# Expert retrieval in a hybrid diffusion layer: index masks from one VectorE comparison, in place of a GpSimd subtraction and two ScalarE steps

## The chip, the cores and the metric

The kernel runs on one core of a Trainium2 chip. The metric is the device time of one execution, in microseconds (us). Three runs of the kernel before took 3352.09, 3352.52 and 3352.99 us; the median is 3352.52 us.

The engines are named as the profile names them: PE is TensorE (matmuls), DVE is VectorE, ACT is ScalarE, POOL is GpSimd, SP is SyncE.

## The reference

The program computes one layer over 512 latent tokens of width 2048 with 256 context tokens: modulated RMS norm, a combined projection into attention heads and gated short convolutions, an output projection with a gated residual, and then a product-key retrieval of experts. The change lies in the retrieval, which the reference computes like this, for blocks of 128 tokens:

```python
def block(hb):                                           # PEER_HEADS = 8, PEER_TOPK = 16, N_KEYS = 128
    q = (hb @ w_pq).reshape(nb, PEER_HEADS, 2, PEER_QDIM // 2)
    s = jnp.einsum('nhpd,hpkd->nhpk', q, sub_keys).astype(jnp.float32)
    s_top, i_top = lax.top_k(s, PEER_TOPK)
    cand = s_top[:, :, 0, :, None] + s_top[:, :, 1, None, :]
    cand_idx = i_top[:, :, 0, :, None] * N_KEYS + i_top[:, :, 1, None, :]
    best_s, best_pos = lax.top_k(cand.reshape(nb, PEER_HEADS, PEER_TOPK * PEER_TOPK), PEER_TOPK)
    expert = jnp.take_along_axis(cand_idx.reshape(nb, PEER_HEADS, PEER_TOPK * PEER_TOPK), best_pos, axis=-1)
    gate = jax.nn.softmax(best_s, axis=-1).astype(hb.dtype).reshape(nb, PEER_HEADS * PEER_TOPK)
    expert = expert.reshape(nb, PEER_HEADS * PEER_TOPK)
    act = jax.nn.gelu(jnp.einsum('nd,ned->ne', hb, u_tab[expert]), approximate=False) * gate
    return jnp.einsum('ne,ned->nd', act, v_tab[expert])
```

The step that changes is `take_along_axis`: for each of the 16 best candidates of a head it picks the expert's index.

## The kernel before

Each fp32 product is made of three matmuls (`mm3`, L106 to L109): weights come as tiles of 128 x 1024 fp32, ACT rounds them to a high part `whi` (L102), DVE subtracts to get the low part `wlo` (L103), and PE needs both. There are four buffers each for `raw`, `whi` and `wlo`. The `wlo` of one half tile of every second query is made on POOL in place of DVE (the argument `eng` in `query`).

The retrieval begins about 1063 us into the span. There are 16 queries, two for each of 8 heads. `query(c)` makes 128 features of one half of a head for all 512 tokens (PE, 48 matmuls of 512 columns into `qps`), `half_top` multiplies them with the 128 sub-keys (`scp`, L556), copies the scores to SBUF on ACT (`sc`, L558), and finds the 16 best of each token with the DVE's max, index and replace instructions (L563 to L567). `head_top` adds the two halves' values and indices for the 50 pairs that can be among the 16 best (L582; NP = 50), finds the 16 best pairs (L590 to L594), and has their positions as floats in `posf` (L595). All this is done for four groups of 128 tokens (t = 0 to 3), tokens on partitions.

To turn a position into an expert's index the kernel makes, for each head and each t, a tile `hit` of 128 x (16 x 50): POOL subtracts the position from an iota 0 to 49 (L599); ACT squares it (L607) and takes max(0, 1 - x) (L608), which is 1 where the position matches and 0 elsewhere; POOL multiplies with the candidates' indices `cidx`, the second half of `both` (L609); DVE sums over the 50 (L613). In the loop at the end of the section, the subtraction of a head is issued with its `head_top`, `hit_masks` two queries later, and `hit_sums` a query after that. The order of instructions on each engine is set by the framework's scheduler, under the marks `issue_after`; each engine then runs its list in that order. There are eight `hit` buffers, two heads' worth.

After the queries PE goes on to 128 blocks of dense scores against the table u (`u_block`, 48 matmuls of 352 columns into `sps`, two tiles of `wlo` each), the first few of them still in the same loop, while DVE finishes the last heads and the softmax of the gates (`gates`, L616 to L625). Expert indices of the last 160 tokens go to POOL, which gathers rows by indirect DMA (L728). The rest of the program, some 2000 us, goes over the tables u and v at the pace of PE.

Of the kernel before, what the change touches and what calls it, by code (L numbers as in the profile page):

```python
# [10 lines left out]
F32 = mybir.dt.float32  # L11
# [3 lines left out]
AF = mybir.ActivationFunctionType  # L15
ALU = mybir.AluOpType
# [4 lines left out]
P = 128  # L21
# [18 lines left out]
NP = len(PAIRS)  # L40


def build(nc, tc, ap, es):
# [269 lines left out]
    with pool("att", side="right", **reuse) as att:  # L313
        bias = [att.tile([P, 512], F32, name=f"bias{i}") for i in range(2)]
# [194 lines left out]
    iota = pq.tile([P, P], F32, name="iota")  # L509
# [4 lines left out]
    tk = tks.enter_context(pool("tk", side="right", **reuse))  # L514

    gate = {}
    mark = {}

    def u_block():
        i = u_block.n  # L520
        u_block.n += 1
        ps = psum("u", "sps", P, ND)
        for hf in range(2):
            w = weights(ap["uT"][i, hf])
            for k in range(8):
                kk = 8 * hf + k
                mm = mm3(ps, (w[0][:, k, :], w[1][:, k, :]), (HH[:, kk, 0:ND], HL[:, kk, 0:ND]), kk == 0, kk == KD - 1)
        mark["pe"], mark["dve"], mark["act"] = mm, weights.lo, weights.hi
        if i % 2 == 0:
            u_block.out = uo.tile([P, 2, ND], F32, tag="ug", bufs=2, name="ug")  # L530
        nc.scalar.activation(u_block.out[:, i % 2, :], ps, AF.Gelu)
        if i % 2 == 1:
            nc.scalar.dma_start(gu[i // 2], u_block.out)
# [3 lines left out]
    def query(c):  # L537
        ps = psum("query", "qps", P, T)
        for hf in range(2):
            w = weights(ap["wpq"][c, hf], nc.gpsimd if c % 2 == 1 and hf == 0 else None)  # L540
            for k in range(8):
                kk = 8 * hf + k
                mm = mm3(ps, (w[0][:, k, :], w[1][:, k, :]), h2[kk], kk == 0, kk == KD - 1)
            if hf == 0:
                gate["pe"] = mm
        qt = tk.tile([P, T], F32, tag="qt", bufs=3, name="qt")
        gate["act"] = nc.scalar.activation(qt, ps, AF.Copy)
        sk = tk.tile([P, P], F32, tag="sk", bufs=3, name="sk")
        nc.sync.dma_start(sk, ap["skT"][:, c, :])
        return qt, sk  # L550

    def half_top(p, qt, sk):
        sp = psum("scores", "scp", P, 4, P)
        with tc.issue_after(gate["pe"].ins):
            for t in range(4):
                nc.tensor.matmul(sp[:, t, :], qt[:, P * t:P * t + P], sk, start=True, stop=True)  # L556
        sc = tk.tile([P, 4, P], F32, tag="sc", bufs=2, name="sc")
        nc.scalar.activation(sc, sp, AF.Copy)  # L558
        tops = tk.tile([P, 2, 4, 16], F32, tag=f"top{p}", bufs=2, name="tops")
        top = tops[:, 0]  # L560
        idx = tk.tile([P, 4, 16], U32, tag=f"idx{p}", bufs=2, name="idx")
        for t in range(4):
            nc.vector.max(top[:, t, 0:8], sc[:, t, :])  # L563
            nc.vector.max_index(idx[:, t, 0:8], top[:, t, 0:8], sc[:, t, :])
            nc.vector.match_replace(sc[:, t, :], top[:, t, 0:8], sc[:, t, :], NEG)
            nc.vector.max(top[:, t, 8:16], sc[:, t, :])
            nc.vector.max_index(idx[:, t, 8:16], top[:, t, 8:16], sc[:, t, :])  # L567
        if p == 0:
            nc.vector.tensor_scalar(tops[:, 1], idx, P, None, op0=ALU.mult)
        else:  # L570
            nc.vector.tensor_copy(tops[:, 1], idx)
        return tops

    def head_top(hd, first, second):
        both = tk.tile([P, 2, 4, NP], F32, tag="cand", bufs=2, name="both")
        o = 0
        for a in range(9):
            n, na = (16 // (a + 1), 1) if a < 8 else (1, 8)
            dst = both[:, :, :, o:o + n * na]
            x = second[:, :, :, 0:n].to_broadcast([P, 2, 4, n * na]) if na > 1 else second[:, :, :, 0:n]  # L580
            y = first[:, :, :, a:a + na].to_broadcast([P, 2, 4, n * na]) if n > 1 else first[:, :, :, a:a + na]
            nc.vector.tensor_tensor(dst, x, y, op=ALU.add)  # L582
            o += n * na
        cand, cidx = both[:, 0], both[:, 1]
        assert o == NP
        pos = tk.tile([P, 4, 16], U32, tag="pos", bufs=2, name="pos")
        posf = tk.tile([P, 4, 16], F32, tag="posf", bufs=2, name="posf")
        for t in range(4):
            bt = best[:, t, hd, :]
            nc.vector.max(bt[:, 0:8], cand[:, t, :])  # L590
            nc.vector.max_index(pos[:, t, 0:8], bt[:, 0:8], cand[:, t, :])
            nc.vector.match_replace(cand[:, t, :], bt[:, 0:8], cand[:, t, :], NEG)
            nc.vector.max(bt[:, 8:16], cand[:, t, :])
            nc.vector.max_index(pos[:, t, 8:16], bt[:, 8:16], cand[:, t, :])  # L594
        nc.vector.tensor_copy(posf, pos)  # L595
        hits = [None] * 4
        for t in (3, 2, 1, 0):
            hit = tk.tile([P, 16, NP], F32, tag="hit", bufs=8, name="hit")
            nc.gpsimd.tensor_tensor(hit, iota[:, 0:NP].unsqueeze(1).to_broadcast([P, 16, NP]),  # L599
                                    posf[:, t, :].unsqueeze(2).to_broadcast([P, 16, NP]), op=ALU.subtract)  # L600
            hits[t] = hit
        return hd, hits, cidx

    def hit_masks(hd, hits, cidx):
        for t in (3, 2, 1, 0):
            with tc.issue_after(gate["act"].ins):
                nc.scalar.activation(hits[t], hits[t], AF.Square)  # L607
            nc.scalar.activation(hits[t], hits[t], AF.Relu, bias=1.0, scale=-1.0)  # L608
            nc.gpsimd.tensor_tensor(hits[t], hits[t], cidx[:, t, :].unsqueeze(1).to_broadcast([P, 16, NP]), op=ALU.mult)  # L609

    def hit_sums(hd, hits, cidx):
        for t in (3, 2, 1, 0):
            nc.vector.tensor_reduce(expt[:, t, hd, :], hits[t], axis=AX.X, op=ALU.add)  # L613

    def gates():
        for t in range(4):  # L616
            bt = best[:, t]
            mx = pq.tile([P, NH], F32, tag="mx", bufs=2, name="mx")
            nc.vector.tensor_copy(mx, bt[:, :, 0])
            nc.vector.tensor_tensor(bt, bt, mx.unsqueeze(2).to_broadcast([P, NH, 16]), op=ALU.subtract)  # L620
            nc.scalar.activation(bt, bt, AF.Exp)
            sm = pq.tile([P, NH], F32, tag="sm", bufs=2, name="sm")
            nc.vector.tensor_reduce(sm, bt, axis=AX.X, op=ALU.add)
            nc.vector.reciprocal(sm, sm)
            nc.vector.tensor_tensor(bt, bt, sm.unsqueeze(2).to_broadcast([P, NH, 16]), op=ALU.mult)  # L625
# [3 lines left out]
    found = summed = None  # L629
    for c in range(1, 2 * NH + 4):  # L630
        nxt = None
        if c < 2 * NH:
            nxt = query(c)
        else:
            for _ in range(2):
                u_block()
            gate["act"], gate["pe"] = mark["act"], mark["pe"]
        if c == 2 * NH + 1:
            gates()
            u_block()  # L640
        if c % 2 == 1:
            if summed:
                hit_sums(*summed)
            summed = None
        elif found:
            hit_masks(*found)
            summed, found = found, None
        if c <= 2 * NH:
            halves.append(half_top((c - 1) % 2, *qs))
            qs = nxt  # L650
            if c % 2 == 0:
                if c == 2 * NH:
                    u_block()
                found = head_top(c // 2 - 1, *halves)
                halves = []
# [303 lines left out]
```

## Time and profile before

| what | value |
|---|---|
| median of the three runs | 3352.52 us |
| the profiled execution's own time | 3354.18 us |
| its span (first to last instruction) | 3352.3 us |
| PE busy | 3251.0 us, 97% of the span |
| DVE busy | 2494.3 us, 74% |
| ACT busy | 1180.7 us, 35% |
| POOL busy | 674.7 us, 20% |

PE is busy in nearly all of the span, so a stretch is of interest where it is not. A row of the timeline gives start (us from the span's start), duration, engine, line, operation, output and inputs, shapes and count; in square brackets stands how long the engine sat idle before it, and what ended that. An instruction that has started but can't get at its operands shows as a longer duration, not as idle time.

### The profile page before, as it was taken

The page shows a single profiled execution, that of the slowest core. Times are in us where ns is not written, and L with a number is a line of the kernel's source. Part 1 is how long each engine was busy: PE and PEld are TensorE (multiplying, and loading weights), DVE is VectorE, ACT ScalarE, POOL GpSimd, SP SyncE. Part 2 cuts the span into 40 slices and gives each one's busy share as a digit, 9 for nine tenths or more (in the row PEclk, how much of TensorE's full clock was granted, in tenths as well). Part 3 has the DMA queues.
Part 4 walks back from the last instruction along what each step waited for, and adds up shares of the span by engine and source line. Part 5 has one row for each costly group of instructions (what it writes and reads, how often), then busy time and mean ns, then how long its engine had stood idle before and what let it go on. Part 6 is the DMA issues. An engine that isn't in the chain of part 4 may idle for free.

```text
span 3352.3 us, 48155 instructions
## 1 busy us (share of the span) xinstructions
PE 3251.0 (97%) x18951; PEld 2994.3 (89%) x18951; DVE 2494.3 (74%) x3648; ACT 1180.7 (35%) x1584; POOL 674.7 (20%) x400
## 2 busy tenths in 40 slices
PE   4899999999999998999999999999999999999999
PEld 1488888878887888999999999999999999999999
DVE  4444444888756798888788788667688899889885
ACT  3344444322323445333333333323333333333332
POOL 0000000000000465121122221222233333333330
PEclk9999999999999999999999999999999999999999
DMA  8722221788773323889999999998999999999994
GB/s 301 250 68 65 65 62 57 253 276 281 243 251 117 105 86 127 318 330 353 341 346 344 339 336 347 350 351 337 361 357 363 381 369 364 372 377 364 366 346 169
DMA packets 265315, 912.52 MB, mean 272 GB/s; under 512 B 23808, under 2 KB 77312, under 8 KB 222720
## 3 DMA queue, kind: packets, MB, share of 16 engines
q1 hardware_dynamic: 208208, 527.74, 45.1%
q0 software_dynamic: 46080, 335.56, 25.9%
q10 hardware_dynamic: 10800, 46.14, 3.4%
q8 instruction: 149, 2.44, 0.3%
q14 instruction: 78, 0.64, 0.1%
HBM read 854.82 MB, written 54.53 MB: 271 GB/s over the span
## 4 chain that ended last, share of the span: by engine, by line
PE 83%; DMA 8%; DVE 5%; POOL 2%; issue 2%; ACT 1%; SPq 0%; DVEq 0%; ACTq 0%; POOLq 0%
PE sps L107 8%; PE sps L109 8%; PE sps L108 8%; PE ops L107 7%; PE ops L109 7%; PE ops L108 7%; PE xps L107 4%; PE xps L109 4%; PE xps L108 4%; DMA raw<-wada 3%; PE hps L107 2%; PE hps L109 2%; PE hps L108 2%; PE gps L714 2%; DMA row<-u,exi 2%; PE yps L107 2%
## 5 line engine op out<-in xcount | busy, mean ns | idle before, releaser
L102 ACT ACTIVATE whi<-raw 128x1024 fp32r<-128x1024 f32 x672 | 709.7, 1058 | 1558.0 <-PE sps L108 398.4
L103 DVE TENSOR_TENSOR wlo<-raw,whi 128x1024 fp32r<-128x1024 f32 x664 | 819.1, 1249 | 308.0 <-ACT whi L102 280.2
L109 PE MATMUL sps<-HH,wlo 128*128 128x352 f32 x2048 | 664.4, 324 | 18.4 <-DVE wlo L103 18.3
L107 PE MATMUL sps<-HH,whi 128*128 128x352 f32 x2048 | 670.8, 328 | 0.0
L108 PE MATMUL sps<-HL,whi 128*128 128x352 f32 x2048 | 662.9, 324 | 0.0
L107 PE MATMUL ops<-Ah,whi 128*128 128x352 f32 x1536 | 497.4, 324 | 5.3 <-ACT whi L102 5.3
L108 PE MATMUL ops<-Al,whi 128*128 128x352 f32 x1536 | 493.2, 321 | 0.0
L109 PE MATMUL ops<-Ah,wlo 128*128 128x352 f32 x1536 | 493.2, 322 | 0.0
L728 POOL DMA_INDIRECT row<-v,exi x160 | 325.3, 2033 | 611.1 <-DVE h2row L753 447.2
L109 PEld LDWEIGHTS sps<-HH,wlo 128*128 128x128 f32 x2048 | 387.1, 189 | 21.3 <-DVE wlo L103 21.3
L107 PEld LDWEIGHTS sps<-HH,whi 128*128 128x128 f32 x2048 | 387.6, 189 | 0.0
L108 PEld LDWEIGHTS sps<-HL,whi 128*128 128x128 f32 x2048 | 387.6, 189 | 0.0
L728 POOL DMA_INDIRECT row<-u,exi x160 | 208.8, 1305 | 789.6 <-DVE row L742 705.3
L742 DVE SCALAR_TENSOR_TENSOR row<-row,h2row 128x2048 f32<-128x2048 f32 x128 | 292.1, 2288 | 72.1 <-DMA row<-u,exi 72.0
L107 PE MATMUL xps<-HH,whi 128*128 128x512 f32 x768 | 306.6, 399 | 2.0 <-ACT whi L102 2.0
L109 PE MATMUL xps<-HH,wlo 128*128 128x512 f32 x768 | 303.9, 396 | 0.0
L108 PE MATMUL xps<-HL,whi 128*128 128x512 f32 x768 | 303.6, 395 | 0.0
L753 DVE SCALAR_TENSOR_TENSOR h2row<-row,dots,h2row 128x2048 f32<-128x2048 f32 x127 | 298.0, 2346 | 0.7 <-DMA row<-v,exi 0.7
L107 PEld LDWEIGHTS ops<-Ah,whi 128*128 128x128 f32 x1536 | 289.2, 188 | 5.6 <-ACT whi L102 5.6
L108 PEld LDWEIGHTS ops<-Al,whi 128*128 128x128 f32 x1536 | 289.6, 189 | 0.0
L109 PEld LDWEIGHTS ops<-Ah,wlo 128*128 128x128 f32 x1536 | 288.6, 188 | 0.6 <-DVE wlo L103 0.2
L103 POOL TENSOR_TENSOR wlo<-raw,whi 128x1024 fp32r<-128x1024 f32 x8 | 19.8, 2481 | 1004.2 <-ACT whi L102 1004.2
(276 smaller groups left out, 5005.3 us busy)
## 6 DMA issues: line engine op xcount, KB each, us to landing
raw<-uT SPq DMA_DIRECT2D x256, 512.0 KB, 6.4
raw<-vb SPq DMA_DIRECT2D x256, 512.0 KB, 8.4
raw<-wada SPq DMA_DIRECT2D x192, 512.0 KB, 4.9
raw<-win SPq DMA_DIRECT2D x96, 512.0 KB, 4.5
gu<-ug ACTq DMA_DIRECT2D x64, 352.0 KB, 6.2
gd<-stg ACTq DMA_DIRECT2D x11, 2048.0 KB, 10.7
gt<-gd SPq DMA_DIRECT2D x32, 704.0 KB, 8.8
gl<-gu SPq DMA_DIRECT2D x32, 704.0 KB, 9.0
```

What stands on the lines that cost most here:

```text
L102: weights.hi = nc.scalar.activation(hi, raw, AF.Copy)
L103: weights.lo = (eng or nc.vector).tensor_tensor(lo, raw, hi.bitcast(F32), op=ALU.subtract)
L107: nc.tensor.matmul(ps, lw[0], rw[0], start=start, stop=False)
L108: nc.tensor.matmul(ps, lw[0], rw[1], start=False, stop=False)
L109: return nc.tensor.matmul(ps, lw[1], rw[0], start=False, stop=stop)
L714: nc.tensor.matmul(gps[:, j, :], oj[:, j, :], oi[:, j, :], start=True, stop=True)
L728: nc.gpsimd.indirect_dma_start(out=row.rearrange("p k d -> p (k d)"), out_offset=None, in_=ap[tab], in_offset=bass.IndirectOffsetOnAxis(ap ...
L742: nc.vector.scalar_tensor_tensor(row, row, 1.0, h2row if s < P else h2ext, op0=ALU.mult, op1=ALU.mult, accum_out=dots[:, s:s + 1])
L753: nc.vector.scalar_tensor_tensor(ag, row, dots[:, s:s + 1], ag, op0=ALU.mult, op1=ALU.add)
```

## The change

Lines L599, L607 and L608 go. DVE compares the iota with the positions in one instruction per t (`is_equal`, 1 or 0 as a float), written right behind `posf` in `head_top`, and POOL's multiplication is issued directly behind each comparison. `hit_masks` is gone; `hit_sums` stays where it was in the loop.

```diff
         nc.vector.tensor_copy(posf, pos)
         hits = [None] * 4
         for t in (3, 2, 1, 0):
-            hit = tk.tile([P, 16, NP], F32, tag="hit", bufs=8, name="hit")
-            nc.gpsimd.tensor_tensor(hit, iota[:, 0:NP].unsqueeze(1).to_broadcast([P, 16, NP]),
-                                    posf[:, t, :].unsqueeze(2).to_broadcast([P, 16, NP]), op=ALU.subtract)
-            hits[t] = hit
+            hits[t] = tk.tile([P, 16, NP], F32, tag="hit", bufs=8, name="hit")
+            nc.vector.tensor_tensor(hits[t], iota[:, 0:NP].unsqueeze(1).to_broadcast([P, 16, NP]),
+                                    posf[:, t, :].unsqueeze(2).to_broadcast([P, 16, NP]), op=ALU.is_equal)
+            nc.gpsimd.tensor_tensor(hits[t], hits[t], cidx[:, t, :].unsqueeze(1).to_broadcast([P, 16, NP]), op=ALU.mult)
         return hd, hits, cidx
-
-    def hit_masks(hd, hits, cidx):
-        for t in (3, 2, 1, 0):
-            with tc.issue_after(gate["act"].ins):
-                nc.scalar.activation(hits[t], hits[t], AF.Square)
-            nc.scalar.activation(hits[t], hits[t], AF.Relu, bias=1.0, scale=-1.0)
-            nc.gpsimd.tensor_tensor(hits[t], hits[t], cidx[:, t, :].unsqueeze(1).to_broadcast([P, 16, NP]), op=ALU.mult)
...
         elif found:
-            hit_masks(*found)
             summed, found = found, None
```

In the new program the multiplication is L601, the sum L606, and lines further down are 7 or 8 lower. The instructions' order on the engines moves at three places.

On DVE, behind the search for the best pairs of one of the middle heads (`tops`, `idx` and `sc` belong to the next head's first half), before:

```order
L594 MAX_INDEX pos<-best,both 128x8 x2
L564 MAX_INDEX idx<-tops,sc 128x8
L595 CAST posf<-pos 128x64
L563 MAX tops<-sc 128x8
L565 MATCH_REPLACE sc<-tops,sc 128x128
L564 MAX_INDEX idx<-tops,sc 128x8
```

and now:

```order
L594 MAX_INDEX pos<-best,both 128x8 x2
L595 CAST posf<-pos 128x64
L599 TENSOR_TENSOR hit<-iota,posf 128x800 x4
L103 TENSOR_TENSOR wlo<-raw,whi 128x1024
L563 MAX tops<-sc 128x8 x2
L564 MAX_INDEX idx<-tops,sc 128x8 x2
```

Four comparisons stand ahead of the next half's search, with one `wlo` behind them.

On DVE, at the last head, where the softmax of the gates begins (`mx`, `sm`), before:

```order
L595 CAST posf<-pos 128x64
L619 COPY mx<-best 128x8 x2
L103 TENSOR_TENSOR wlo<-raw,whi 128x1024
L620 TENSOR_TENSOR best<-best,mx 128x128 x2
L619 COPY mx<-best 128x8 x2
L620 TENSOR_TENSOR best<-best,mx 128x128 x2
```

and now:

```order
L595 CAST posf<-pos 128x64
L612 COPY mx<-best 128x8 x2
L599 TENSOR_TENSOR hit<-iota,posf 128x800 x4
L613 TENSOR_TENSOR best<-best,mx 128x128 x2
L612 COPY mx<-best 128x8
L103 TENSOR_TENSOR wlo<-raw,whi 128x1024
L613 TENSOR_TENSOR best<-best,mx 128x128
L612 COPY mx<-best 128x8
L606 TENSOR_REDUCE expt<-hit 128x16
L616 TENSOR_REDUCE sm<-best 128x8
L613 TENSOR_TENSOR best<-best,mx 128x128
L617 RECIPROCAL sm<-sm 128x8
```

The four comparisons and the head's four sums now stand among the gates' instructions, ahead of the second `wlo` that follows `posf`; before, the sums stood behind five more `wlo`.

On POOL, for the last heads up to the first gathers, before:

```order
L599 TENSOR_TENSOR hit<-iota,posf 128x800 x4
L609 TENSOR_TENSOR hit<-hit,both 128x800 x4
L599 TENSOR_TENSOR hit<-iota,posf 128x800 x4
L609 TENSOR_TENSOR hit<-hit,both 128x800
L728 DMA row<-u,exi 128x2048
L609 TENSOR_TENSOR hit<-hit,both 128x800 x3
L728 DMA row<-u,exi 128x2048 x159
```

and now:

```order
L601 TENSOR_TENSOR hit<-hit,both 128x800 x4
L103 TENSOR_TENSOR wlo<-raw,whi 128x1024
L601 TENSOR_TENSOR hit<-hit,both 128x800 x12
L720 DMA row<-u,exi 128x2048 x160
```

Half of POOL's `hit` instructions are gone, and the first gather stands behind all multiplications.

## Rows read from the trace of the kernel before

**Rows 1.** Busy time by stretch: us, each engine's busy time, clock, DMA.

```profile
1105.00:1270.00 165.00, 162.21 (x772) 136.09 (x771) 147.26 (x721) 80.14 (x104) 102.55 (x54) 0.99 0.29 85
1270.00:1310.00 40.00, 30.95 (x168) 29.79 (x168) 37.79 (x182) 16.63 (x20) 14.84 (x8) 0.87 0.31 102
```

**Rows 2.** Waits of PE, 1105 to 1350: us in total, times, longest.

```profile
PE sps L109 <- DVE wlo L103: 9.0, 4, 4.8
PE scp L556 <- ACT sc L558: 2.8, 3, 1.9
```

**Rows 3.** Timeline of PE: scores of two queries, a half block, the last wait.

```profile
1105.30 1.06 PE L556 MATMUL scp<-sk,qt 128*128 128x128 f32 x8
1117.11 1.06 PE L556 MATMUL scp<-sk,qt 128*128 128x128 f32 x8
...
1267.74 0.32 PE L107 MATMUL sps<-HH,whi 128*128 128x352 f32 x1
1271.58 0.32 PE L107 MATMUL sps<-HH,whi 128*128 128x352 f32 x1
...
1302.70 0.43 PE L109 MATMUL sps<-HH,wlo 128*128 128x352 f32 x1 [1.68 <-DVE wlo L103]
```

**Rows 4.** Timeline of POOL: the four subtractions of heads 0, 5, 6 and 7.

```profile
1120.09 6.94 POOL L599 TENSOR_TENSOR hit<-iota,posf 128x800 f32<-128x800 f32 x4 [4.88 <-DVE posf L595]
...
1253.90 7.00 POOL L599 TENSOR_TENSOR hit<-iota,posf 128x800 f32<-128x800 f32 x4 [8.56 <-DVE posf L595]
1279.85 6.97 POOL L599 TENSOR_TENSOR hit<-iota,posf 128x800 f32<-128x800 f32 x4 [11.00 <-DVE posf L595]
1310.59 7.53 POOL L599 TENSOR_TENSOR hit<-iota,posf 128x800 f32<-128x800 f32 x4 [15.90 <-DVE mx L619]
```

**Rows 5.** Timeline of DVE: first instructions of the steps of one head.

```profile
1216.44 0.48 DVE L563 MAX8 tops<-sc 128x8 f32<-128x128 f32 x2
...
1221.13 0.97 DVE L613 TENSOR_REDUCE expt<-hit 128x16 f32<-128x800 f32 x1
1222.01 0.18 DVE L571 CAST tops<-idx 128x64 f32<-128x64 uint32 x1
1222.11 1.22 DVE L103 TENSOR_TENSOR wlo<-raw,whi 128x1024 fp32r<-128x1024 f32 x1
1223.24 1.12 DVE L582 TENSOR_TENSOR both<-tops 128x128 f32<-128x128 f32 x9
...
1224.48 0.31 DVE L590 MAX8 best<-both 128x8 f32<-128x50 f32 x2
...
1227.63 0.07 DVE L564 MATCH_VALUE_LOAD idx<-tops,sc 128x8 f32 x1
```

**Rows 6.** DVE groups, 1360 to 1500: a comparison of the same kind; busy, mean ns.

```profile
L700 DVE TENSOR_TENSOR HH<-iota,ijt 128x512 fp32r<-128x512 f32 x17 | 11.7, 687 | 0.0
```

**Rows 7.** Groups of DVE, 1105 to 1350: busy, mean ns | idle before.

```profile
L613 DVE TENSOR_REDUCE expt<-hit 128x16 f32<-128x800 f32 x32 | 31.4, 980 | 20.4 <-POOL hit L609 20.4
```

**Rows 8.** Timeline of DVE and POOL where their two-input instructions meet.

```profile
1235.11 1.76 POOL L609 TENSOR_TENSOR hit<-hit,both 128x800 f32<-128x800 f32 x1
1235.12 2.83 DVE L103 TENSOR_TENSOR wlo<-raw,whi 128x1024 fp32r<-128x1024 f32 x1
...
1089.16 3.09 POOL L103 TENSOR_TENSOR wlo<-raw,whi 128x1024 fp32r<-128x1024 f32 x1 [0.24 <-ACT whi L102]
1089.91 3.42 DVE L103 TENSOR_TENSOR wlo<-raw,whi 128x1024 fp32r<-128x1024 f32 x1
...
1310.59 2.95 POOL L599 TENSOR_TENSOR hit<-iota,posf 128x800 f32<-128x800 f32 x1 [15.90 <-DVE mx L619]
1311.64 0.48 DVE L620 TENSOR_TENSOR best<-best,mx 128x128 f32<-128x128 f32 x2
...
1333.43 6.09 DVE L103 TENSOR_TENSOR wlo<-raw,whi 128x1024 fp32r<-128x1024 f32 x1 [1.65 <-ACT whi L102]
```

**Rows 9.** Timeline of DVE: the first `wlo` behind the gates.

```profile
1320.24 1.22 DVE L103 TENSOR_TENSOR wlo<-raw,whi 128x1024 fp32r<-128x1024 f32 x1
```

## The prediction

> **What bounds the kernel now.** I read the page's slices first: PE is the long engine nearly everywhere, so only a stretch in which PE stands still can give time back, and only one in which it will stand still longer can cost any. Then I took the stretch of the retrieval apart by windows. From 1105 to 1270 us PE is busy 162.2 of 165 us and DVE 147.3; from 1270 to 1310 PE falls to 31.0 of 40 while DVE has 37.8 [rows 1]. So DVE is the engine behind PE's gaps. The view of waits says the same: PE waits 9.0 us for `wlo`, which DVE makes, and 2.8 us for `sc` [rows 2]. The last such wait ends at 1302.70 [rows 3]; from there PE runs without a gap.
>
> PE's own pace through a head is two queries of 11.8 us (scores at 1105.30 and 1117.11), 23.6 us [rows 3]. DVE and POOL go round in 25.95 us (POOL's bursts of heads 5 and 6 start at 1253.90 and 1279.85) [rows 4]. So DVE falls behind PE by some 2 us per head, PE's lead runs out toward the end of the queries, and PE then waits for DVE.
>
> **What DVE does per head.** From issue to issue [rows 5]: one half's search takes 1221.13 - 1216.44 = 4.69 us, twice 9.38; a sum 0.88, four 3.52; a `wlo` 1.13, three 3.39; the pairs 1.12 less 0.08 of overlap, 1.04; their search 1227.63 - 1224.48 = 3.15; three small conversions some 0.35. That is 20.8 us of work without any waiting. The rest of the 25.95 are waits: for POOL's products (20.4 us over the stretch [rows 7]), and hidden ones inside instructions, which are what decides here.
>
> **The hidden ones.** At 1235.12 a `wlo` takes 2.83 us [rows 8] and not 1.22 as at 1222.11 [rows 5]; POOL's product that started 0.01 us earlier took 1.76 [rows 8]. The two were done one after the other: 1.7 us of the 2.83 is DVE standing still. DVE's sums are not lengthened, though 19 of the 32 had waited for one product and ran beside the next: their mean is 0.98 [rows 7], and one with POOL idle took 0.97 [rows 5]. So a DVE instruction with two inputs in SBUF, like `wlo`, and a POOL instruction on SBUF exclude each other.
>
> **The change part by part.**
>
> ACT loses 64 instructions and POOL 32. Neither is PE's bound; the scores' copy `sc` no longer stands behind squares that wait for POOL, so the 2.8 us of that wait [rows 2] can go.
>
> DVE gains 32 comparisons of 128 x 800 with two SBUF inputs. The trace has no such size. The comparison of the same kind with 512 columns takes 687 ns [rows 6], the `wlo` with 1024 takes 1.22 us [rows 5]; between them 800 columns come to 0.69 + 288 x 0.53/512 = 0.99, issue to issue 0.9 us. Four are 3.6 us per head: 20.8 + 3.6 = 24.4 us, already over PE's 23.6.
>
> POOL's four products now start while DVE still compares. The first may run as soon as the first comparison has ended, when DVE is in its second. Who goes next, each time, is the open cost. From above: POOL gets its turn after each comparison it has waited for, and the third and fourth comparison and the `wlo` behind them each wait for one product, 3 x 1.7 = 5.1 us; a fourth meeting would make 6.8. From below: DVE keeps on through its five instructions, and no comparison waits. The trace has both. At 1089.16 POOL's `wlo` waits under a DVE `wlo`; the next DVE `wlo`, issued at 1089.91 right behind, takes 3.42 us, so POOL went between [rows 8]. At 1310.59 POOL's subtraction waits under a `wlo` and, by its 2.95 us (the other three of its burst take (7.53 - 2.95)/3 = 1.53 [rows 4, 8]), also under the two small subtractions L620 that follow in 0.48 us: DVE went on [rows 8]. At 1333.43 a `wlo` even stands 6.09 us, through three products. I take POOL's turn after each: the first case is the one with tiles of this size. Each of the three waits takes the place of nothing that goes: what goes is the wait for products at the sums, since the last of them now ends at 9.8 + 1.8 = 11.6 us behind the positions (comparisons and `wlo` with their waits 3.6 + 1.1 + 5.1 = 9.8), and DVE comes to the sums at 9.8 + 4.7 = 14.5.
>
> The Trainium skill ("SBUF — State Buffer", section "Who interferes with whom") says that a VectorE instruction with two SBUF inputs contends with a GpSimd instruction that reads SBUF, and that whichever issued first has the shared pair for the whole instruction while the other blocks fully. The 2.83 us agree. Read strictly by order of issue, the rule would let POOL in after the second comparison and so on, which is my 5.1 us; by it the two L620 should not have gone ahead, so the trace differs from it there.
>
> **The sum.** Per head 24.4 + 5.1 = 29.5 us. Head 0's positions are ready at 1120.0, as before, since nothing ahead of them changes. Head 6's come at 1120.0 + 6 x 29.5 = 1297 against 1279.8 [rows 4]: 17 us late. From there the last head holds, by the new order on DVE: comparisons with two waits 7.0; a search 4.7; two `wlo` and a conversion 2.4; a sum 0.9; a `wlo` 1.1; three sums 2.6; two `wlo` 2.3; a search 4.7; a `wlo`, the pairs, their search and a `wlo` 6.6. That is 32.3, so positions of head 7 at 1329.3, against 1310.5.
>
> Then comes the place that decides, as `wlo` are what PE eats there. Before, `wlo` number six from the one that ended PE's last wait is ready at 1320.24 + 1.22 = 1321.46 [rows 9]; PE takes 3.84 us per half block (1271.58 - 1267.74) [rows 3], so it came to that one at 1302.70 + 5 x 3.84 = 1321.9, with 0.5 us to spare. In the new order, between head 7's positions and the same `wlo` stand: comparisons with two waits 7.0; two subtractions behind the last two products 3.6; a `wlo` 1.1; four sums 3.5; the small steps of the softmax some 3; the `wlo` itself 1.2. Ready at 1329.3 + 19.4 = 1348.7, against the 1321.9 at which PE would want it. PE is 27 us later there. Behind it nothing gives that back: the four sums are done earlier than before, but PE had no waits left behind 1302.70.
>
> The profiled execution took 3354.18 us (its span 3352.3); 3354.18 + 27 = 3381. The median of the runs shown is 1.66 us lower: **3380 us**. Taking PE's lower clock after longer gaps into account (0.87 in 1270 to 1310 [rows 1]) could add a few us.
>
> **The rivals.**
>
> *DVE keeps its turn.* Comparisons and `wlo` go through, the products run beside the search, and only the small conversion behind it waits for the last product, some 1.5 us. Period 25.9, head 6 at 1275.4, head 7 at 1275.4 + 32.3 - 3.4 + 1.7 = 1306, then 19.4 - 3.4 + some 2 more for gates behind products = 18: the deciding `wlo` at 1324 against 1321.9. Time 3352.5 + 2 = 3355, no change. For it: the 1311.64 row. Against: 1089.91.
>
> *The period falls to the work itself.* Nothing meets, or POOL's products slip wholly under the searches: 24.4 per head, head 6 at 1266.4, head 7 some 29 later at 1295.4, the deciding `wlo` at 1295.4 + 12.4 = 1308. Then PE's 11.8 us of waits [rows 2] go, with part of the lost clock: 3338 to 3345, faster. It decides from the point where DVE waits less than about 1 us per head for POOL. For it: 20.4 us of waits at sums vanish, and POOL and ACT give up half of their part. Against: every two-input meeting in rows 8 costs somebody its full length, and the new order puts both parties side by side.
>
> *Mixed turns.* POOL gets in once or twice per head and DVE goes on for the rest: 1.7 to 3.4 us less per head than the forecast, over six heads 10 to 20, and up to 3.4 less in each of the last two bursts of comparisons. Of the 27 us some 4 to 13 are left: about 3362. Both rows 8 together speak for it.
>
> **How the numbers follow.** POOL's turn after each, 0.53; mixed 0.15; DVE keeps its turn 0.17; faster 0.15. A change under 0.2% (6.7 us) can't be told from none. The forecast and three quarters of the mixed case are slower: 0.53 + 0.12 = 0.65. The rest of it and the second case are the same: 0.20. Faster: 0.15. The forecast's own range goes from a wait or two less in the last bursts and heads (some 8 us less) to a fourth meeting per head (6 x 1.7 = 10 us more): 3372 to 3391. The whole range leaves out most of the faster case at one end and a little of the other: 3350 to 3391.
>
> **What the profile after would show.** Comparisons of 0.99 us where they meet nothing and near 2.7 where they wait, about two per head; `wlo` behind them near 2.8. Sums without idle time before them. The products' first starts 29.5 us apart. PE's waits for `wlo` some 35 us in place of 9. Wrong it would be if comparisons all take about 1 us while POOL's products are the long ones: then DVE keeps its turn. If comparisons alone exceed 1.1 us where no product runs, the size was misjudged.

## The result: about one per cent slower, as forecast

The changed kernel takes 3384.36 us (median of 6 runs, 3380.97 to 3394.44), the kernel before 3352.35 us (6 runs, 3350.03 to 3352.99). The ratio is 1.0100, with a 95% interval of 1.0088 to 1.0113. The forecast was 3380 us, in a range of 3350 to 3391. The profiled execution of the changed kernel took 3381.62 us; its span is 3379.8 us.

### The profile page after: what moved, and what is told of

It is laid out like the page before. It is cut to its first block, busy times and chain, and to the rows that moved or that the text cites. A ratio compares the mean times of both kernels' runs of the same rounds, so it can differ in the third digit from the quotient of the medians.

```text
span 3379.8 us, 48092 instructions
## 1 busy us (share of the span) xinstructions
PE 3260.2 (96%) x18951; PEld 3000.7 (89%) x18951; DVE 2534.6 (75%) x3680; ACT 1131.8 (33%) x1520; POOL 637.7 (19%) x368
## 4 chain that ended last, share of the span: by engine, by line
PE 82%; DVE 9%; DMA 7%; issue 1%; ACT 1%; SPq 0%; DVEq 0%; ACTq 0%
PE sps L109 9%; PE sps L107 9%; PE sps L108 9%; PE ops L107 7%; PE ops L109 7%; PE ops L108 7%; PE xps L107 4%; PE xps L108 4%; PE xps L109 4%; DMA raw<-wada 3%; PE hps L107 2%; PE hps L109 2%; PE hps L108 2%; PE gps L706 2%; DVE wlo L103 2%; PE yps L107 2%
## 5 line engine op out<-in xcount | busy, mean ns | idle before, releaser
L109 PE MATMUL sps<-HH,wlo 128*128 128x352 f32 x2048 | 666.4, 325 | 26.7 <-DVE wlo L103 26.7
L109 PE MATMUL ops<-Ah,wlo 128*128 128x352 f32 x1536 | 493.4, 322 | 0.0
L109 PEld LDWEIGHTS sps<-HH,wlo 128*128 128x128 f32 x2048 | 388.8, 190 | 29.3 <-DVE wlo L103 29.3
L109 PE MATMUL xps<-HH,wlo 128*128 128x512 f32 x768 | 304.0, 396 | 0.0
L109 PEld LDWEIGHTS ops<-Ah,wlo 128*128 128x128 f32 x1536 | 289.1, 188 | 0.5 <-DVE wlo L103 0.2
```

What stands on the lines that cost most here:

```text
L109: return nc.tensor.matmul(ps, lw[1], rw[0], start=False, stop=stop)
```

## The profile after

First the stretches of [rows 1] again, and one more behind them. Columns: stretch, its length, busy time of PE, PE's weight loads, DVE, ACT and POOL (with counts), granted clock of PE, DMA share, GB/s.

```profile
1105.00:1270.00 165.00, 149.03 (x670) 121.85 (x669) 163.90 (x661) 37.12 (x48) 69.18 (x28) 0.96 0.23 74
1270.00:1310.00 40.00, 24.89 (x124) 22.61 (x123) 39.86 (x158) 8.01 (x9) 14.49 (x7) 0.85 0.20 59
1310.00:1350.00 40.00, 35.14 (x205) 34.56 (x205) 39.80 (x124) 16.41 (x21) 11.89 (x6) 0.93 0.45 148
```

DVE is now busy in 163.90 of 165 us (147.26 before), and PE in 149.03 (162.21 before). Busy is not the same as working: the DVE rows below hold its standing still. PE's waits of 1105 to 1350, as in [rows 2]:

```profile
PE sps L109 <- DVE wlo L103: 18.8, 4, 11.0
PE qps L109 <- DVE wlo L103: 17.1, 8, 2.8
```

PE waits 35.9 us for `wlo` (9.0 before). The wait for `sc` (2.8 before) is gone. The next rows are one head on DVE, the fourth, from the start of its comparisons to the `wlo` behind them:

```profile
1204.87 0.99 DVE L599 TENSOR_TENSOR hit<-iota,posf 128x800 f32<-128x800 f32 x1
1205.78 0.98 DVE L599 TENSOR_TENSOR hit<-iota,posf 128x800 f32<-128x800 f32 x1
1206.68 2.55 DVE L599 TENSOR_TENSOR hit<-iota,posf 128x800 f32<-128x800 f32 x1
1209.16 2.56 DVE L599 TENSOR_TENSOR hit<-iota,posf 128x800 f32<-128x800 f32 x1
1211.64 2.75 DVE L103 TENSOR_TENSOR wlo<-raw,whi 128x1024 fp32r<-128x1024 f32 x1
```

and the same time on POOL:

```profile
1205.94 2.44 POOL L601 TENSOR_TENSOR hit<-hit,both 128x800 f32<-128x800 f32 x1 [17.34 <-DVE hit L599]
1208.34 2.53 POOL L601 TENSOR_TENSOR hit<-hit,both 128x800 f32<-128x800 f32 x1
1210.83 2.48 POOL L601 TENSOR_TENSOR hit<-hit,both 128x800 f32<-128x800 f32 x1
1213.27 2.75 POOL L601 TENSOR_TENSOR hit<-hit,both 128x800 f32<-128x800 f32 x1
```

Read the two fences against each other. The second comparison runs from 1205.78 to 1206.76. The first product starts at 1205.94 and ends at 1208.38: it stands 0.8 us behind that comparison and then works for 1.6 us. The third comparison, issued at 1206.68, ends at 1209.23: it stands until the product is through, and then works. So it goes on, one turn each, down to the `wlo`. The third and fourth comparison and the `wlo` are 1.57, 1.58 and 1.53 us too long, 4.7 us in all. The third and fourth comparison wait like this in all eight heads (2.51 to 2.56 us). Behind them stands a `wlo` in the first six heads, in the seventh a search, which does not wait, and in the last small subtractions, which do. The groups of DVE, 1105 to 1350 (busy, mean ns | idle before), answer to [rows 7]:

```profile
L599 DVE TENSOR_TENSOR hit<-iota,posf 128x800 f32<-128x800 f32 x32 | 54.6, 1766 | 0.2
L606 DVE TENSOR_REDUCE expt<-hit 128x16 f32<-128x800 f32 x32 | 29.8, 969 | 0.0
```

The 20.4 us of idle time ahead of the sums are gone. In their place the comparisons, 0.98 us by themselves, have a mean of 1.77 us. POOL's bursts give the pace (heads 0, 3, 4, 5, 6 and 7; compare [rows 4]):

```profile
1115.75 10.09 POOL L601 TENSOR_TENSOR hit<-hit,both 128x800 f32<-128x800 f32 x4 [5.90 <-DVE hit L599]
...
1205.94 10.07 POOL L601 TENSOR_TENSOR hit<-hit,both 128x800 f32<-128x800 f32 x4 [17.34 <-DVE hit L599]
...
1235.71 10.07 POOL L601 TENSOR_TENSOR hit<-hit,both 128x800 f32<-128x800 f32 x4 [17.32 <-DVE hit L599]
...
1265.48 10.09 POOL L601 TENSOR_TENSOR hit<-hit,both 128x800 f32<-128x800 f32 x4 [17.34 <-DVE hit L599]
1296.34 8.92 POOL L601 TENSOR_TENSOR hit<-hit,both 128x800 f32<-128x800 f32 x4 [20.77 <-DVE hit L599]
1328.78 9.07 POOL L601 TENSOR_TENSOR hit<-hit,both 128x800 f32<-128x800 f32 x4 [23.52 <-DVE hit L599]
```

A head takes 29.8 us (1235.71 - 1205.94) in place of 25.95. The last head on DVE, from its positions to the `wlo` that decides:

```profile
1327.40 0.19 DVE L595 CAST posf<-pos 128x64 f32<-128x64 uint32 x1
...
1327.65 6.82 DVE L599 TENSOR_TENSOR hit<-iota,posf 128x800 f32<-128x800 f32 x4
1334.40 3.60 DVE L613 TENSOR_TENSOR best<-best,mx 128x128 f32<-128x128 f32 x2
...
1338.00 1.21 DVE L103 TENSOR_TENSOR wlo<-raw,whi 128x1024 fp32r<-128x1024 f32 x1
...
1345.44 1.22 DVE L103 TENSOR_TENSOR wlo<-raw,whi 128x1024 fp32r<-128x1024 f32 x1
```

Two subtractions of the gates, 0.24 us each before (0.48 for two in [rows 8]), take 3.60 us, as each stands behind a product. PE's last waits in that stretch:

```profile
1339.26 0.42 PE L109 MATMUL sps<-HH,wlo 128*128 128x352 f32 x1 [1.52 <-DVE wlo L103]
...
1346.71 0.66 PE L109 MATMUL sps<-HH,wlo 128*128 128x352 f32 x1 [3.34 <-DVE wlo L103]
```

and three short stretches, behind the first of these waits, behind the second, and after that (columns as above):

```profile
1339.30:1343.20 3.90, 3.90 (x24) 3.78 (x24) 3.90 (x10) 3.25 (x7) 0.00 (x0) 1.00 0.67 222
1346.70:1353.50 6.80, 6.79 (x25) 6.79 (x26) 4.82 (x11) 0.00 (x0) 0.77 (x1) 0.55 0.95 354
1353.50:1360.00 6.50, 6.50 (x42) 6.50 (x41) 2.45 (x2) 2.47 (x3) 0.00 (x0) 1.00 0.97 381
```

Behind the last wait PE has work all the time, but a clock of 0.55 for 6.8 us, near the lower of its two levels (1.2 of 2.4 GHz). That costs 6.8 x 0.45 = 3.1 us. PE makes up none of its delay later: the 3001st matmul of L109 starts at 2045.25, and at 2017.65 in the kernel before.

## The experiments

Theory A is the prediction's: DVE's instructions with two inputs and POOL's products wait for each other, by turns. Theory B: the loss is DVE's added work. Theory C: it is the new order of the last head. "Positions" is the time from head 0's conversion L595 (`posf`) to head 7's in each trace, which leaves out how early the execution came to head 0.

| kernel | median us | median of before beside it | ratio, 95% interval | positions, head 0 to 7 |
|---|---|---|---|---|
| before | 3352.35 | | | 190.4 |
| changed | 3384.36 | 3352.35 | 1.0088 to 1.0113 | 213.0 |
| e1 no products | 3350.14 | 3352.08 | 0.9981 to 1.0000 | 183.3 |
| e2 products on DVE | 3382.68 | 3352.08 | 1.0068 to 1.0102 | 217.0 |
| e3 meant to be reversed | 3385.31 | 3352.08 | 1.0083 to 1.0117 | 213.4 |
| e4 last head as before | 3377.26 | 3352.08 | 1.0056 to 1.0090 | 213.4 |
| e5 products last first | 3361.62 | 3354.77 | 1.0014 to 1.0033 | 191.6 |
| e6 comparisons spread | 3365.93 | 3354.77 | 1.0021 to 1.0048 | 197.1 |
| e7 spread, old last head | 3359.34 | 3354.77 | 1.0004 to 1.0023 | 197.1 |
| e8 before, sums later | 3343.20 | 3354.77 | 0.9952 to 0.9979 | 180.7 |
| e9 e5 and e4 together | 3355.31 | 3353.11 | 0.9997 to 1.0015 | 191.7 |

### e1: the changed kernel without POOL's products

```diff
-            nc.gpsimd.tensor_tensor(hits[t], hits[t], cidx[:, t, :].unsqueeze(1).to_broadcast([P, 16, NP]), op=ALU.mult)
```

> The changed kernel without POOL's products: the sums count matches in place of adding indices, so every gathered row and one-hot is that of index 1. Theory A (the comparisons and the wlo behind them each wait for one product): three waits of some 1.57 us per head go, a head takes 29.8 - 4.7 = 25.1 us on DVE, the comparisons take 0.98 us each; the last head loses two more waits of the gates. Some 30 us less than the changed kernel: about 3352, between 3347 and 3360. Theory B (DVE's own added work, 3.6 us per head, makes the loss, and the waits would otherwise be filled by others): within 8 us of the changed kernel, 3376 or more. Theory C (the new order at the last head makes it): also within 8 us of it.

3350.14 us: the whole loss is gone with the products, though all of the change's DVE work is still there. So B alone can't make the loss. C is not settled by this run, as the last head has lost its products too (e4 tries it). And since every index is 1 here, what follows the retrieval gathers other rows than the changed kernel does; e5 and e9 keep the products. A head of DVE in this trace:

```profile
1170.95 3.70 DVE L599 TENSOR_TENSOR hit<-iota,posf 128x800 f32<-128x800 f32 x4
1174.56 1.22 DVE L103 TENSOR_TENSOR wlo<-raw,whi 128x1024 fp32r<-128x1024 f32 x1
```

Four comparisons take 3.70 us (6.84 in the changed kernel). Positions are 25.1 us apart in heads 0 to 3: DVE's work without any product, 21.5 us and 3.6 us of comparisons. The three steps behind them take 26.1 to 26.4 us: two hold a meeting with POOL's own `wlo`, the third one more `wlo` of DVE.

PE still waits 11.0 us for `wlo` in this run, and 8.82 of them for one that stands behind the comparisons of the seventh head and the search that follows them:

```profile
1274.76 3.70 DVE L599 TENSOR_TENSOR hit<-iota,posf 128x800 f32<-128x800 f32 x4
...
1283.06 1.20 DVE L103 TENSOR_TENSOR wlo<-raw,whi 128x1024 fp32r<-128x1024 f32 x1
...
1284.32 0.66 PE L109 MATMUL sps<-HH,wlo 128*128 128x352 f32 x1 [8.82 <-DVE wlo L103]
```

It is PE's last wait for DVE there; behind the last head PE has none.

### e2: the products on DVE

```diff
-            nc.gpsimd.tensor_tensor(hits[t], hits[t], cidx[:, t, :].unsqueeze(1).to_broadcast([P, 16, NP]), op=ALU.mult)
+            nc.vector.tensor_tensor(hits[t], hits[t], cidx[:, t, :].unsqueeze(1).to_broadcast([P, 16, NP]), op=ALU.mult)
```

> The four products of a head run on DVE instead of POOL: 3.6 us more work per head on DVE, but nothing of POOL left to meet except its own wlo. Theory A: a head takes 25.1 + 3.6 = 28.7 us, up to 1.5 more where POOL's wlo meets a product, against 29.8 now; the gates at the last head wait for nothing: 3372 to 3386, the same as the changed kernel or up to 12 us less. Theory B: 3.6 us more per head over eight heads, 3384 + 25 to 29 = 3409 to 3413.

3382.68 us, in A's range; B's 3409 to 3413 falls. That it is the time of the changed kernel is in part chance. A step with three `wlo`, as in the changed kernel, takes 28.4 us here (to heads 1 and 5) in place of 29.8: DVE does 3.6 us more work and waits 4.7 us less. But the order of DVE's `wlo` is another one as well. In every head but the last, one stands behind the next half's search and none directly behind the comparisons, and in the fourth head PE waits 15.94 us for it:

```profile
1216.88 1.21 DVE L103 TENSOR_TENSOR wlo<-raw,whi 128x1024 fp32r<-128x1024 f32 x1
...
1218.14 0.79 PE L109 MATMUL qps<-HH,wlo 128*128 128x512 f32 x1 [15.94 <-DVE wlo L103]
```

The step to the next head takes 39.0 us. So within a head POOL takes nothing off DVE in the changed kernel: its four products cost DVE more (4.7 us of waits) than if DVE made them (3.6). What the move would do to the whole time with the `wlo` in their old places, this run doesn't show.

### e3: the products in reversed order (first try)

```diff
+        for t in (0, 1, 2, 3):
             nc.gpsimd.tensor_tensor(hits[t], hits[t], cidx[:, t, :].unsqueeze(1).to_broadcast([P, 16, NP]), op=ALU.mult)
```

The sums on DVE are reversed too.

> POOL takes the tiles in reverse, so its first product needs the last comparison, and all four comparisons run before any product; the sums are reversed too. The same work on both engines. Theory A: no comparison waits, all take 0.98 us; the wlo behind them waits at most once (1.6 us) and the small conversion behind the search at most once (1.5 us): 1.6 to 4.7 us less per head, so 11 to 30 us less in all, about 3365 (3354 to 3373). Theory B and C: no change against the changed kernel, 3380 to 3390.

3385.31 us, no better. The edit had not reached the engine. The second and third comparison of a head on DVE:

```profile
1211.00 0.99 DVE L599 TENSOR_TENSOR hit<-iota,posf 128x800 f32<-128x800 f32 x1
1211.90 2.55 DVE L599 TENSOR_TENSOR hit<-iota,posf 128x800 f32<-128x800 f32 x1
```

and POOL's first product:

```profile
1211.16 2.44 POOL L602 TENSOR_TENSOR hit<-hit,both 128x800 f32<-128x800 f32 x1 [17.34 <-DVE hit L599]
```

It starts during the second comparison, when only the tile compared first is ready, so that is the one it works on: POOL's products still stood in the order of the comparisons. The run says nothing for or against A, and its expectation of 3365 us is a miss of the edit. It does show that the reversed sums alone change nothing. e5 repeats it with the order held.

### e4: the last head's masks as before

```diff
-            nc.vector.tensor_tensor(hits[t], iota[:, 0:NP].unsqueeze(1).to_broadcast([P, 16, NP]),
-                                    posf[:, t, :].unsqueeze(2).to_broadcast([P, 16, NP]), op=ALU.is_equal)
+            last = hd == NH - 1
+            (nc.gpsimd if last else nc.vector).tensor_tensor(
+                hits[t], iota[:, 0:NP].unsqueeze(1).to_broadcast([P, 16, NP]),
+                posf[:, t, :].unsqueeze(2).to_broadcast([P, 16, NP]), op=ALU.subtract if last else ALU.is_equal)
+            if not last:
...
+            if found[0] == NH - 1:
+                hit_masks(*found)
```

> Heads 0 to 6 as in the changed kernel, head 7 with POOL's subtraction and ACT's square and clip as in the kernel before, so its comparisons, sums and the gates are ordered as before. Theory A: the seven heads have already cost 22 us; what goes is the last head's 6.8 us of comparisons and the 3.3 us by which gates wait, of which PE's waits of 1.5 and 3.3 us behind it show: 5 to 11 us less than the changed kernel, 3373 to 3379. Theory C (the last head's order makes the loss): back to 3352 to 3358.

3377.26 us, 25 us over before in place of 32. The last head's new order is a part of the loss, 7 us, and not its cause (C falls). The other seven heads are as long as in the changed kernel (213.4 us to head 7).

### e5: the tile compared last is multiplied first

```diff
-            nc.gpsimd.tensor_tensor(hits[t], hits[t], cidx[:, t, :].unsqueeze(1).to_broadcast([P, 16, NP]), op=ALU.mult)
+        first = None
+        for t in (0, 1, 2, 3):
+            with tc.issue_after(first.ins) if first else ExitStack():
+                first = nc.gpsimd.tensor_tensor(hits[t], hits[t], cidx[:, t, :].unsqueeze(1).to_broadcast([P, 16, NP]), op=ALU.mult)
```

The sums are reversed as in e3.

> The changed kernel, with GpSimd's four products of a head held in the reversed order: the product of the tile that is compared last runs first, so that none can run until all four comparisons are through (in the run before it that was meant to do this, the products stood in the old order). Theory A (a VectorE instruction with two inputs waits for a GpSimd product that runs when it comes, and the two take turns): all four comparisons 0.98 us; the plain wlo behind them, or the next instruction with two inputs, waits for one product, 1.6 us at most, and where a second stands behind it for one more. So 1.6 to 4.7 us less for each head than the changed kernel, seven heads and the last: 3352 + 32 - (11 to 33) = 3352 to 3373, most likely 3365. Rival D (the length comes from the comparisons themselves, or from four operations of each engine in a row whatever their order): comparisons 3 and 4 stay at 2.5 us or the waits come back in full behind them, 3379 to 3388.

3361.62 us, of a forecast 3352 to 3373. The same instructions, in another order on POOL, and 25 of the 32 us are gone (e3 has the reversed sums without this gain). A head on DVE:

```profile
1201.45 3.70 DVE L599 TENSOR_TENSOR hit<-iota,posf 128x800 f32<-128x800 f32 x4
1205.07 1.22 DVE L103 TENSOR_TENSOR wlo<-raw,whi 128x1024 fp32r<-128x1024 f32 x1
...
1210.89 0.97 DVE L609 TENSOR_REDUCE expt<-hit 128x16 f32<-128x800 f32 x1
1211.77 1.33 DVE L569 TENSOR_SCALAR tops<-idx 128x64 f32<-128x64 uint32 x1
```

and on POOL:

```profile
1205.23 7.83 POOL L604 TENSOR_TENSOR hit<-hit,both 128x800 f32<-128x800 f32 x4 [16.04 <-DVE hit L599]
1213.01 2.39 POOL L103 TENSOR_TENSOR wlo<-raw,whi 128x1024 fp32r<-128x1024 f32 x1
```

No comparison waits. The one `wlo` had been issued ahead of the first product, and it is POOL that waits there. Products two to four run beside DVE's search, which they do not lengthen. What still waits is a small conversion, 1.33 us in place of 0.18. Positions are 26.2 us apart in four of six steps (28.0 and 27.3 in the others): e1's 25.1 and that 1.15.

### e6: the comparisons spread through the next head

```diff
-            nc.vector.max_index(idx[:, t, 8:16], top[:, t, 8:16], sc[:, t, :])
+            seen = nc.vector.max_index(idx[:, t, 8:16], top[:, t, 8:16], sc[:, t, :])
+            if waiting and t in (1, 3):
+                with tc.issue_after(seen.ins):
+                    hit_one(*waiting.pop(0))
...
+        waiting.extend((t, hits, posf, cidx) for t in (3, 2, 1, 0))
+        if hd == NH - 1:
+            while waiting:
+                hit_one(*waiting.pop(0))
```

`hit_one` holds one comparison and its product; it is called in `half_top`, behind the search of tiles 1 and 3.

> The changed kernel, with the four comparisons of each head but the last apart from each other: one behind each pair of searches of the next head (about 2.5 us of search between two of them, or two sums), so that each product finds VectorE in instructions with one input. The comparisons of the last head stay four in a row. Theory A: comparisons 0.98 us, products 1.73 us, nothing waits in heads 0 to 6 but now and then one of the small additions behind the last product (under 1 us); a head then has 21.5 us of work and 3.6 us of comparisons, 25.1 to 26 us, as long as the head of the kernel before (25.95), and only the last head's 7 us (run e4) are left: 3359 (3354 to 3366). Rival B (the comparisons' own work on VectorE makes the loss): 28.8 us more in VectorE less what is hidden, 3376 or more. Rival D (products of 2.4 to 2.7 us and comparisons of 2.5 us wherever they stand): 3379 to 3388.

3365.93 us, at the upper end of A's 3354 to 3366; the central 3359 was too low. Middle heads are 28.0 us, not 25.1 to 26. On DVE:

```profile
1191.38 2.80 DVE L607 TENSOR_TENSOR hit<-iota,posf 128x800 f32<-128x800 f32 x1
...
1195.10 1.07 DVE L585 TENSOR_TENSOR both<-tops 128x128 f32<-128x128 f32 x1
```

and on POOL:

```profile
1190.92 2.41 POOL L103 TENSOR_TENSOR wlo<-raw,whi 128x1024 fp32r<-128x1024 f32 x1
...
1194.26 1.76 POOL L609 TENSOR_TENSOR hit<-hit,both 128x800 f32<-128x800 f32 x1 [0.93 <-DVE hit L607]
```

The expectation had left out POOL's own `wlo`, once per head: the third comparison came 0.46 us behind it and stood 1.8 us. A product then lengthened the first of the pairs by 0.8. 25.1 + 1.8 + 0.8 = 27.7, close to the 28.0. These meetings are of A's kind; the list of POOL's instructions was not complete.

### e7: e6 with the last head as before

```diff
+        if hd < NH - 1:
+            waiting.extend((t, hits, posf, cidx) for t in (3, 2, 1, 0))
+        else:
+            for t in (3, 2, 1, 0):
+                nc.gpsimd.tensor_tensor(hits[t], iota[:, 0:NP].unsqueeze(1).to_broadcast([P, 16, NP]),
+                                        posf[:, t, :].unsqueeze(2).to_broadcast([P, 16, NP]), op=ALU.subtract)
```

`hit_masks` stands behind the last head, as in e4.

> As e6, and the last head's masks as in the kernel before (GpSimd's subtractions, ScalarE's squares and clips, products from GpSimd). Theory A: the last head's 7 us go too, 3352 (3347 to 3358): the whole loss is undone while seven heads of eight have the change's comparisons. Rival C' (what e4 gave back had to do with the back-log of the seven heads before, not with the last head by itself): no more than 3 us under e6.

3359.34 us, a little over the forecast 3347 to 3358, but 6.6 us under e6. Head 7's positions come 197.1 us behind head 0's here, 213.0 in the changed kernel, so the last head has its price with most of the back-log gone (C' falls; e9 repeats it with 191.7). It is 4.6 us over before, not 0. The heads are as long as in e6, so the meetings found there are the likely reason; no run takes them away by themselves.

### e8: the kernel before, with the sums later

```diff
+            gate["dve"] = nc.vector.max_index(idx[:, t, 8:16], top[:, t, 8:16], sc[:, t, :])
...
-        for t in (3, 2, 1, 0):
-            nc.vector.tensor_reduce(expt[:, t, hd, :], hits[t], axis=AX.X, op=ALU.add)
+        with tc.issue_after(gate["dve"].ins):
+            for t in (3, 2, 1, 0):
+                nc.vector.tensor_reduce(expt[:, t, hd, :], hits[t], axis=AX.X, op=ALU.add)
...
-            if summed:
+            if summed and c > 2 * NH:
                 hit_sums(*summed)
-            summed = None
+                summed = None
...
             qs = nxt
+            if c % 2 == 1 and summed:
+                hit_sums(*summed)
+                summed = None
```

> The kernel before, with one edit: the four sums of a head (VectorE) issued behind the first half's search of the next head but one, not ahead of it, so that VectorE doesn't stand idle for GpSimd's products (20.4 us of idle time ahead of the sums in the profile of before). It tests how much of a head's 25.95 us in the kernel before is such waiting. If VectorE's waiting sets the head: up to 2.5 us less a head, until TensorE's own 24.5 us or so set it, and TensorE's waits of 9.0 + 2.8 us go: 3340 to 3345. Rival: TensorE bounds these heads anyway (it is busy for 162 of 165 us) and its waits come from elsewhere (the end of the last head): 3350 to 3354, no change.

3343.20 us: faster than both kernels (0.9966 of before, 0.9952 to 0.9979). The first stretch of [rows 1] in it:

```profile
1105.00:1270.00 165.00, 165.00 (x803) 140.31 (x803) 156.84 (x777) 78.68 (x104) 102.53 (x54) 1.00 0.30 92
```

its group of sums on DVE, 1105 to 1350:

```profile
L614 DVE TENSOR_REDUCE expt<-hit 128x16 f32<-128x800 f32 x32 | 30.1, 970 | 2.2 <-POOL hit L609 2.2
```

and PE's waits for DVE and ACT, 1105 to 1350:

```profile
PE sps L109 <- DVE wlo L103: 2.7, 3, 1.2
PE sps L107 <- ACT whi L102: 1.8, 1, 1.8
```

PE is busy for all of the 165 us. The idle time ahead of the sums is 2.2 us (20.4 before), PE's waits 4.5 (11.8). Middle heads come every 24.0 us (25.8 before), close to the 23.6 of PE's two queries [rows 3]. In the kernel before, DVE's waiting for products set the head.

### e9: e5 and e4 together

Seven heads with e5's edit, the last with e4's.

> Runs e5 and e4 together: seven heads with the change's comparisons and GpSimd's products with the tile that is compared last ahead, the last head's masks as in the kernel before. It asks whether the loss is the sum of the two parts and of nothing else. Theory A (the waits of comparisons and of the wlo for products cost 24 to 25 us, the last head 7): e5's 1.0024 less 7 us in 3353 (0.21%), 1.0003 (0.9985 to 1.0020), so no loss that can be told; positions 26.2 us apart as in e5. Rival (the 64 instructions that ScalarE lost or the 28.8 us of comparisons cost something by themselves that e5 hid): a rest of 6 us or more, 1.002 and over.

3355.31 against 3353.11 us, 1.0006 (0.9997 to 1.0015): no loss that can be told. Seven heads out of eight have the change's comparisons on DVE, ScalarE has lost 56 of the 64 instructions, and the time is that of before. Within the interval, which reaches to 5 us, the loss is the sum of the waits in seven heads and of the last head's order.

## Why the prediction was right, step by step

- *DVE bounds the gaps.* Held. PE's waits in the changed kernel are all for `wlo`. e8 shows it from the other side: less waiting on DVE, and PE's gaps close.
- *DVE's work of 20.8 us a head and 3.6 us of comparisons.* The comparisons are 0.99 and 0.98 us, 0.90 from issue to issue, as interpolated between [rows 5] and [rows 6]. The rest is 21.5 (e1: 25.1 - 3.6), 0.7 more than added up.
- *POOL's turn after each, three waits of 1.7 us.* Held in heads 0 to 5, where the two cases of [rows 8] had left it open, and with the two waits that were foretold in heads 6 and 7. The choice between those cases was a bet at 0.53, as the prediction says. The waits are 1.57, 1.58 and 1.53, together 4.7 and not 5.1. e1 (no products) and e5 (products later) show that these meetings, not the work, make the loss.
- *29.5 us a head.* 29.8 between heads 1 and 5; the two errors above nearly cancel, which is luck. The first head step took 30.6, as one more `wlo` met POOL's own (the pair at 1132.49 takes 3.20 us, 2.35 in later heads), and the sixth 30.8, as it holds four `wlo` and not three (the fourth at 1290.56). So head 6 comes 20.8 us later than before, counted from head 0 (1294.98 - 1114.45 against 1279.53 - 1119.82), not 17. This is the term that was too small.
- *The last head.* 32.4 us (forecast 32.3), and from its positions to the end of the deciding `wlo` 1346.66 - 1327.40 = 19.3 (forecast 19.4). Before, the latter was 1321.46 - 1310.26 = 11.2. e4, e7 and e9 show the price by itself: 5 to 7 us by the medians over the kernel before beside them (32.0 - 25.2, 11.2 - 4.6 and 6.9 - 2.2).
- *The place that decides.* The `wlo` ends at 1346.66, forecast 1348.7. It is the same one: 1688 matmuls of L109 stand ahead of PE's wait for it, and in the trace of before PE starts the next at 1322.01, where the prediction had worked out 1321.9. But this execution came to head 0 at 1114.45, 5.4 us earlier than the profiled one of before. The prediction took head 0 at the same time in both; e4 with the same work ahead of it has 1118.69, e7 1123.49 and e9 1115.47, so this is a difference of executions. From head 0 on, PE is 1346.66 + 5.4 - 1321.9 = 30.1 us later than it would have wanted, where 27 were forecast.
- *The clock.* "A few us" were named and not added: it is 3.1. 30.1 + 3.1 - 5.4 = 27.8, and the spans differ by 27.5. Without the early start 33.2 would be left; the medians differ by 32.0, and the runs of the changed kernel lie 13.5 us apart. The forecast median was 4.4 us too low. The head steps and the clock together make some 6; the rest lies within the spread of the runs.
- *Signs foretold.* PE's waits for `wlo` 35.9 us (some 35); no idle time ahead of sums; bursts 29.8 us apart (29.5); comparisons that wait 2.55 us (near 2.7), the `wlo` behind them 2.75 (near 2.8).
- *The rivals.* DVE keeping its turn and mixed turns both fall with the waits of the third and fourth comparison, which all eight heads have. The faster case had its price wrong besides: e1 is that case, with a head of 25.1 us, yet at 3350 us and not 3338 to 3345. It took PE's 11.8 us of waits as gone; in e1 PE waits 11.0 us, 8.82 of them behind the comparisons of the seventh head, which the price didn't look at. e5 is close to "DVE keeps its turn" (26.2 us a head, forecast 25.9), and 6.9 us over before, where 2 were forecast. There PE's last wait is 4.61 us, behind the last head, and with that head as before (e9) the excess is gone.

## What to carry to other kernels

A consumer on GpSimd that is released tile by tile starts in the middle of its producer's burst on VectorE; where both read two inputs from SBUF, they then took turns here, and the overlap was worth less than nothing: 4.7 us of waits a head for 3.6 us of products (e2). Before moving work, write down what stands beside it on the other engine, all of it (e6 forgot one instruction), and hold the consumer back until the burst is through: e5 gave back 25 of 32 us by an order alone. And idle time in front of a sum that nobody needs yet is removed by issuing the sum later (e8), without touching the masks.

## What the runs showed of the hardware

In the bursts of the changed kernel the turns are strict: while both engines had such instructions ready, the other one went next: the third and fourth comparison stood through one product each in 8 heads of 8. The `wlo` of [rows 8] that stood through three products (6.09 us at 1333.43) doesn't fit that; why it lost its turn was not tried. An instruction needs no second input to wait: the small conversion L569, 0.18 us by itself, takes 1.33 beside a product in e5, while sums (0.97) and searches run beside products unchanged. The Trainium skill ("SBUF — State Buffer", section "Who interferes with whom") lists `tensor_scalar` and `cast` among the operations that can take the shared pair of ports, when their operands meet certain conditions, and `tensor_reduce` as one that never does on this chip; both agree with these rows.

PE's clock stayed at 1.00 behind a wait of 1.52 us, and was 0.55 for 6.8 us behind one of 3.34 us that began 4.1 us later (1346.71 - 3.34 against 1339.26). So some of what a late `wlo` cost here came after the wait.
